# HGRN2 layer on one core: near-token products done elementwise and summed by a matmul with ones behind the value projections, and the K and Q updates of both directions in one operation each

## The chip, the cores and the metric

The kernel runs on one core of a Trainium2 chip. The metric is the device time of one execution in microseconds; the time before is the median of three runs. A profile shows one execution, and its span (first to last instruction) is slightly shorter than the time of the same run.

The engines that matter here are TensorE (PE in the profile, with its weight loads as PEld), VectorE (DVE), ScalarE (ACT), GpSimd (POOL) and the DMA queue that SyncE issues (SP).

## The reference

Two layers over 1024 latent tokens and 256 context tokens of width 1024. Layer 0 is a neighbourhood attention beside a bidirectional mLSTM and is not touched. Layer 1, where the change lies, is a bidirectional gated linear recurrence (HGRN2) with 16 heads of key and value width 128:

```python
def _c_mixer(h_lat, h_ctx, w_in, lb, h_norm, w_out, need_ctx):
    ...
        q, f_fwd, f_bwd, i, z = _split_cols(h @ w_in, C_SIZES)
        f = lb + (1.0 - lb) * jax.nn.sigmoid(f_pre.astype(F32))    # k = 1 - f, decay = f
    ...
def _gla_chunkwise(q, k, v, lf, S):            # per direction, in chunks
        b = jnp.cumsum(lfc, axis=2)
        o = jnp.einsum('bhtk,bhkv->bhtv', qc * jnp.exp(b), S)
        pair = jnp.exp(jnp.where(tri, b[:, :, :, None, :] - b[:, :, None, :, :], -jnp.inf))
        a = jnp.einsum('bhtk,bhtsk->bhts', qc, pair * kc[:, :, None, :, :])
        o = o + jnp.einsum('bhts,bhsv->bhtv', a, vc)
        S = jnp.exp(bL[:, :, 0])[..., None] * S + jnp.einsum('bhsk,bhsv->bhkv', kc * jnp.exp(bL - b), vc)
```

For a query token t and a key token s of one chunk the weight is a sum over the 128 key channels of q, k and the product of the decays between s and t. The outputs of both directions are added, normalised per head, gated by SiLU(z) and projected.

## The kernel before

Everything is float32 in memory. Dense projections are exact to about float32 by splitting both operands into a high and a low float32r part and doing three float32r passes for each 128 rows of the contraction (lines 117, 118 and 119); `split` (lines 71 and 72) makes the parts: ScalarE copies the high part, VectorE subtracts. The small matmuls of the recurrence are done in float32, and each of these shows as two passes on PE.

Layer 1 runs over the 16 heads, with these steps for each:

- `hg_proj` (from L756) projects the forget gates of both directions and q, transposed (channels on partitions, tokens along the row). `F` holds the decays of one half of the tokens (512), for both directions; `q` the queries.
- `hg_intra` (from L834) does the two halves, half 1 first. It builds `K` (1 - F, both directions, L841) and `Q` (q times F, both directions, L844), and then calls `hg_level` for seven levels. On level `lev` the blocks have h = 2^lev tokens; the block pairs on either side of a boundary are joined. ScalarE gathers the keys that look across the boundary into `ksel` (L875), TensorE multiplies them with the queries for each of the four chunks of 128 tokens (L880), and VectorE writes the result into `A` under a mask: by multiplication on level 0 (L886), by a predicated copy on the others (L890). Then VectorE moves K and Q on by one block of decay, by four operations on 256 elements (L898), and multiplies the block decays (L900).
- After level 0, `hg_diag` sets the diagonal of `A`: L888 adds the two directions of K, L909 multiplies with q on TensorE, L910 copies under the identity mask.
- At the end of `hg_intra`, K is transposed by TensorE (L859) and copied into `kn` (L861).
- `hg_vz` (from L782) projects the values and z: a context tile first, then eight tiles of 128 tokens (24 passes each, `wz` weights). `v` is copied by ScalarE (L799), z gets a sigmoid (L800) and is multiplied on VectorE (L801). The PSUM tiles of all projections share two buffers (`mm`), and the tile of z has one buffer, which the normalisation of the head before still reads (`gyn`, L953).
- `hg_ctx` builds the state that the context leaves (L810 to L829), and `hg_scan` passes over the eight chunks: backward states (L920, L922), then per chunk the three products that make the output (L932, L933, L934) and the forward state (L937, L939). After every four chunks ScalarE squares (L948), GpSimd takes the root (L142, L144), VectorE scales and gates (L953), TensorE transposes (L956), and ScalarE stores to `gyt` (L958), from where a DMA writes it out.

The framework orders the instructions of each engine when the kernel is built, by its own estimate of the times, and each engine then runs its list strictly in that order, waiting on semaphores. So projections are laid between the small matmuls of the recurrence: the value projections of a head between its levels, the gate and query projections of the next head between the steps of the scan. `t(pool, ..., tag, bufs)` takes a buffer of a tag; an operation that writes a buffer waits until its last reader is done.

Of the kernel before, what the change touches and what calls it, by code (L numbers as in the profile page):

```python
# [9 lines left out]
F32 = mybir.dt.float32  # L10
F32R = mybir.dt.float32r
U8 = mybir.dt.uint8
# [31 lines left out]
class Prog:  # L44
# [789 lines left out]
    def hg_intra(self, st, pool):  # L834
        nc = self.nc
        n = 512
        hv = {}
        for hf in (1, 0):
            F, q = st["F"][hf], st["q"][hf]
            K = self.t(pool, [P, 2, n], F32, "gK", 2)  # L840
            nc.vector.tensor_scalar(out=K, in0=F, scalar1=-1.0, scalar2=1.0, op0=ALU.mult, op1=ALU.add)  # L841
            Q = self.t(pool, [P, 2, n], F32, "gQ", 2)
            for d in range(2):
                nc.vector.tensor_tensor(out=Q[:, 1 - d, :], in0=q, in1=F[:, d, :], op=ALU.mult)  # L844
            A = self.t(pool, [P, 4, P], F32, "gA", 2)
            hv[hf] = dict(Q=Q, A=A, T=F, K=K)
        for lev in range(7):
            for hf in (1, 0):
                self.hg_level(hv[hf], lev, pool)
            if lev == 0:  # L850
                for hf in (1, 0):
                    self.hg_diag(hv[hf], st["q"][hf], pool)
        for hf in (1, 0):
            H = hv[hf]
            H["kn"] = []
            for d in range(2):
                p = self.ps("tr", [P, 4, P])
                for c in range(4):
                    nc.tensor.transpose(p[:, c, :], H["K"][:, d, c * P : (c + 1) * P], self.ident)  # L859
                k_ = self.t(pool, [P, 4, P], F32, "gkn", 4)  # L860
                nc.scalar.copy(k_, p)  # L861
                H["kn"].append(k_)
        return hv


    def hg_level(self, H, lev, pool):
        nc = self.nc
        n, h = 512, 1 << lev
        nb = n // (2 * h)
        K, Q, A, Tt = H["K"], H["Q"], H["A"], H["T"]  # L870
        sel = lambda t: t.rearrange("p d (b s i) -> p d b s i", s=2, i=h)

        pick = lambda t: _skew(t[:, 0, :].rearrange("p (b s i) -> p b s i", s=2, i=h), 2, n)
        ksel = self.t(pool, [P, n], F32, "gksel", 3)
        nc.scalar.copy(ksel.rearrange("p (b s i) -> p b s i", s=2, i=h), pick(K))  # L875
        qp = pick(Q)
        pa = self.ps("s", [P, 4, P])
        nbc = P // (2 * h)
        for c in range(4):
            nc.tensor.matmul(  # L880
                pa[:, c, :].rearrange("p (b s i) -> p b s i", s=2, i=h),
                lhsT=ksel[:, c * P : (c + 1) * P], rhs=qp[:, c * nbc : (c + 1) * nbc], start=True, stop=True,
            )
        if lev == 0:

            nc.vector.tensor_tensor(out=A, in0=pa, in1=self.lmask0.unsqueeze(1).to_broadcast([P, 4, P]), op=ALU.mult)  # L886
            H["ks"] = self.t(pool, [P, n], F32, "gksel", 3)
            nc.vector.tensor_tensor(out=H["ks"], in0=K[:, 0, :], in1=K[:, 1, :], op=ALU.add)  # L888
        else:
            nc.vector.copy_predicated(A, self.lmask[:, lev - 1, :].unsqueeze(1).to_broadcast([P, 4, P]), pa)  # L890
        Tv = Tt.rearrange("p d (b s) -> p d b s", s=2)
        bc = lambda t: t.unsqueeze(2).to_broadcast([P, nb, h])
        Kv, Qv = sel(K), sel(Q)
        for t, i, s, tot in (
            (Kv, 0, 0, Tv[:, 0, :, 1]), (Kv, 1, 1, Tv[:, 1, :, 0]),
            (Qv, 0, 0, Tv[:, 1, :, 1]), (Qv, 1, 1, Tv[:, 0, :, 0]),
        ):
            nc.vector.tensor_tensor(out=t[:, i, :, s, :], in0=t[:, i, :, s, :], in1=bc(tot), op=ALU.mult)  # L898
        Tn = self.t(pool, [P, 2, nb], F32, f"gT{lev}", 2)
        nc.vector.tensor_tensor(out=Tn, in0=Tv[:, :, :, 0], in1=Tv[:, :, :, 1], op=ALU.mult)  # L900
        H["T"] = Tn


    def hg_diag(self, H, q, pool):
        nc = self.nc
        pa = self.ps("s", [P, 4, P])
        for c in range(4):
            s = slice(c * P, (c + 1) * P)
            nc.tensor.matmul(pa[:, c, :], lhsT=H["ks"][:, s], rhs=q[:, s], start=True, stop=True)  # L909
        nc.vector.copy_predicated(H["A"], self.ident8.unsqueeze(1).to_broadcast([P, 4, P]), pa)  # L910

    def hg_scan(self, h, st, halves, S, pool, y):
        nc = self.nc
# [48 lines left out]
    def build(self):  # L962
        tc, nc, a = self.tc, self.nc, self.a
        dma = nc.sync.dma_start
        with ExitStack() as es:
# [130 lines left out]
            with tc.tile_pool(name="op0", bufs=2) as op, ExitStack() as wl:  # L1096
                self.gate_bc(0, op, 2, 1)
                later = []
                w1 = self.wo_half(wl, a["woab"], 0, "left", yp, later)
                for tt in [8, 9, 3, 4, 2, 5, 1, 6, 0, 7]:  # L1100
                    xt = self.t(op, [P, D], F32, "ox", 2)[:, 512:D]
                    self.out_tile(w2, 1, tt, self.yd, self.xin(tt), xt, yp, op, 2, part=acc[:, tt, :])
                    nc.gpsimd.dma_start(out=self.x1[tt * P : (tt + 1) * P, 512:D], in_=xt)
                    for ld in later[:2]:
                        ld()
                    later = later[2:]
                self.zero = self.t(lk, [P, CTX], F32, "gzero", 1)
                nc.vector.memset(self.zero, 0.0)
                self.lmask = self.t(lk, [P, 6, P], U8, "glm8", 1)
                self.lmask0 = self.t(lk, [P, P], F32, "glm0", 1)  # L1110
                self.ident8 = self.t(lk, [P, P], U8, "ident8", 1)
                nc.vector.tensor_copy(self.ident8, self.ident)
                lm = self.t(op, [P, D], F32, "nx", 1)[:, 0 : 7 * P].rearrange("p (l f) -> p l f", f=P)
                dma(out=lm, in_=a["glm"])
                nc.vector.tensor_copy(self.lmask, lm[:, 1:7, :])
                nc.vector.tensor_copy(self.lmask0, lm[:, 0, :])
                self.gate_bc(0, op, 2, 0)
                wr.close()
                right = es.enter_context(ExitStack())
                self.open_h(right)  # L1120
                self.wp = right.enter_context(tc.tile_pool(name="w1", bufs=2, side="right"))
                self.rawp = op
                self.slabs = 4
                wf = self.wring([a["wc"][:, 2048 : 2048 + P]], P)
                for tt in [8, 9, 4, 5, 6, 7, 0, 1, 2, 3]:
                    xt = self.t(op, [P, D], F32, "ox", 2)
                    dma(out=xt[:, 512:D], in_=self.x1[tt * P : (tt + 1) * P, 512:D])
                    self.out_tile(w1, 0, tt, self.yd, self.xin(tt), xt[:, 0:512], op, op, 2)
                    if tt < 8:
                        nc.gpsimd.dma_start(out=self.x1[tt * P : (tt + 1) * P, 0:512], in_=xt[:, 0:512])  # L1130
                    xn = self.t(op, [P, D], F32, "nx", 1)
                    self.norm(xn, xt, op)
                    self.mod_tr(1, [xn], tt, op, self.h_sink(tt * P, P))

            with l1:
                pool = l1.enter_context(tc.tile_pool(name="hg", bufs=2))
                self.rawp = pool
# [172 lines left out]
```

## Time and profile before

| what | value |
|---|---|
| time, median of 3 runs | 3584.57 us (3582.02 to 3586.4) |
| time of the profiled run | 3583.22 us |
| its span | 3581.4 us |
| PE busy | 3516.8 us (98%) |
| DVE busy | 2216.1 us (62%) |
| ACT busy | 1418.4 us (40%) |
| POOL busy | 454.6 us (13%) |
| mean granted TensorE clock | 0.992 |

In the timeline a row gives the start, the duration, the engine, the line and the tiles. The end of a matmul is modelled, and the next one starts before it: what a matmul takes of TensorE is read from the start of one to the start of the next (called its slot here), not from its duration. Operations on VectorE that do not depend on each other overlap a little in the same way.

### The profile page before, as it was taken

Reading aid. Unit: us, or ns where it says so; the run is one execution under the profiler, and the core shown is the slowest. Engines: PE = TensorE matmul, PEld = TensorE weight load, DVE = VectorE, ACT = ScalarE, POOL = GpSimd, SP = SyncE. Lnnn points to the kernel's source line nnn. Section 1 sums busy time; section 2 is a strip of 40 time slices with the busy share of each in tenths; the row PEclk is TensorE's granted clock in tenths of the full one; section 3 lists DMA queues with packets and bytes.
Section 4 is the critical chain, followed back from the end, with each engine's and each line's share of the span. In section 5 each row is a group of like instructions: output and inputs, shape, how many; then the busy total and the mean of one; then the engine's idle time right before and its main releaser. Section 6 shows DMA issues by size and latency. Waiting matters only on the chain.

```text
span 3581.4 us, 65599 instructions
## 1 busy us (share of the span) xinstructions
PE 3516.8 (98%) x24954; PEld 3222.6 (90%) x24954; DVE 2216.1 (62%) x5976; ACT 1418.4 (40%) x3493; POOL 454.6 (13%) x752
## 2 busy tenths in 40 slices
PE   8999999999999999998999999999999999999998
PEld 5879999999999999997788999999999999999877
DVE  4646676666754765664666666666666666666653
ACT  5545555445533434433354333333333333333341
POOL 2222222122211212211010000000000000000000
PEclk9999999999999999999999999999999999999999
DMA  5532323232234434324752111111111111110263
GB/s 206 175 103 75 84 70 84 72 89 75 79 96 148 127 93 141 118 72 141 228 158 62 36 36 36 33 36 36 36 35 34 31 36 36 35 33 27 74 205 116
DMA packets 323051, 305.25 MB, mean 85 GB/s; under 512 B 29016, under 2 KB 280088, under 8 KB 322608
## 3 DMA queue, kind: packets, MB, share of 16 engines
q1 hardware_dynamic: 290704, 217.44, 20.9%
q0 software_dynamic: 32032, 83.61, 6.9%
q8 instruction: 197, 3.23, 0.4%
q14 instruction: 118, 0.97, 0.1%
HBM read 241.49 MB, written 59.30 MB: 84 GB/s over the span
## 4 chain that ended last, share of the span: by engine, by line
PE 88%; issue 5%; DMA 3%; DVE 1%; ACT 1%; POOL 1%; SPq 0%; POOLq 0%; DVEq 0%; ACTq 0%
PE mm L119 18%; PE mm L117 18%; PE mm L118 18%; PE s L880 6%; PE mm L729 2%; PE mm L731 2%; PE mm L730 2%; PE acc L674 2%; PE tr L654 2%; PE acc L458 2%; PE s L467 2%; DMA mld<-md 1%; PE acc L448 1%; PE acc L933 1%; PE s L909 1%
## 5 line engine op out<-in xcount | busy, mean ns | idle before, releaser
L119 PE MATMUL mm<-wh,hl 128*128 128x256 f32 x2560 | 748.9, 293 | 0.2 <-DVE hl L250 0.2
L117 PE MATMUL mm<-wh,hh 128*128 128x256 f32 x2560 | 746.5, 292 | 0.0
L118 PE MATMUL mm<-wl,hh 128*128 128x256 f32 x2560 | 745.4, 291 | 0.0
L119 PEld LDWEIGHTS mm<-wh,hl 128*128 128x128 f32 x2560 | 488.5, 191 | 11.1 <-issue 4.1
L117 PEld LDWEIGHTS mm<-wh,hh 128*128 128x128 f32 x2560 | 488.6, 191 | 7.7 <-issue 1.4
L118 PEld LDWEIGHTS mm<-wl,hh 128*128 128x128 f32 x2560 | 488.7, 191 | 7.1 <-issue 0.8
L117 PE MATMUL mm<-hh,wh 128*128 128x512 f32 (+1 forms) x1216 | 449.5, 370 | 5.9 <-ACT gFc L769 5.9
L118 PE MATMUL mm<-hl,wh 128*128 128x512 f32 (+1 forms) x1216 | 449.2, 369 | 0.0
L119 PE MATMUL mm<-hh,wl 128*128 128x512 f32 (+1 forms) x1216 | 448.7, 369 | 0.0
L119 PE MATMUL mm<-wzh,hl 128*128 128x256 f32 x1024 | 295.3, 288 | 0.0
L117 PE MATMUL mm<-wzh,hh 128*128 128x256 f32 x1024 | 294.2, 287 | 0.0
L118 PE MATMUL mm<-wzl,hh 128*128 128x256 f32 x1024 | 293.9, 287 | 0.0
L875 ACT COPY gksel<-gK 128x512 f32<-128x512 f32 x224 | 148.8, 664 | 317.0 <-PE s L880 159.9
L117 PEld LDWEIGHTS mm<-hh,wh 128*128 128x128 f32 x1216 | 230.3, 189 | 37.5 <-ACT gFc L769 6.2
L119 PEld LDWEIGHTS mm<-hh,wl 128*128 128x128 f32 x1216 | 230.3, 189 | 31.7
L118 PEld LDWEIGHTS mm<-hl,wh 128*128 128x128 f32 x1216 | 230.3, 189 | 30.8
L880 PE MATMUL s<-gQ,gksel 128*128 128x128 f32 x1792 | 254.9, 284 | 0.0
L729 PE MATMUL mm<-woh,yh 128*128 128x512 f32 x576 | 229.8, 400 | 5.6 <-DVE oacc L743 3.5
L880 PEld LDWEIGHTS s<-gQ,gksel 128*128 128x128 f32 x1792 | 231.4, 191 | 1.3
L731 PE MATMUL mm<-woh,yl 128*128 128x512 f32 x576 | 229.6, 399 | 0.8 <-DVE yl L72 0.8
L730 PE MATMUL mm<-wol,yh 128*128 128x512 f32 x576 | 229.3, 398 | 0.4 <-DVE wol L72 0.2
L71 ACT CAST wh<-wraw 128x512 fp32r<-128x512 f32 x240 | 147.2, 619 | 202.8 <-PE mm L118 126.2
(307 smaller groups left out, 7349.6 us busy)
## 6 DMA issues: line engine op xcount, KB each, us to landing
wraw<-yd SPq DMA_DIRECT2D x144, 256.0 KB
wraw<-in_wab_dram SPq DMA_DIRECT2D x112, 256.0 KB
md<-ev POOLq DMA_DIRECT2D x100, 256.0 KB, 2.7
wraw<-in_wc_dram SPq DMA_DIRECT2D x96, 256.0 KB
adar<-in_wada_dram POOLq DMA_DIRECT2D x32, 512.0 KB, 4.8
wraw<-in_wc_dram SPq DMA_DIRECT2D x128, 128.0 KB
adar<-in_wada_dram SPq DMA_DIRECT2D x16, 512.0 KB
wraw<-in_wab_dram SPq DMA_DIRECT2D x64, 128.0 KB
```

The costliest lines, as they stand in the source:

```text
L71: nc.scalar.copy(hi, x)
L117: mm(ps, lhsT=lh(k), rhs=rh(k), start=(k == 0), stop=False)
L118: mm(ps, lhsT=lh(k), rhs=rl(k), start=False, stop=False)
L119: mm(ps, lhsT=ll(k), rhs=rh(k), start=False, stop=(k == nk - 1))
L458: nc.tensor.matmul(num, lhsT=qc[:, j, :], rhs=C[d][:, j, :], start=False, stop=(j == 1))
L467: nc.tensor.matmul(u, lhsT=st["k"][c][:, j * P : (j + 1) * P], rhs=vw, start=True, stop=True)
L654: nc.tensor.transpose(pt[:nk, i, :], pr[:, o : o + nk], self.ident)
L729: mm(ps, lhsT=yh[:, k, :], rhs=w.h(kk), start=(kk == 0), stop=False)
L730: mm(ps, lhsT=yh[:, k, :], rhs=w.l(kk), start=False, stop=False)
L731: mm(ps, lhsT=yl[:, k, :], rhs=w.h(kk), start=False, stop=(kk == 8 * len(qs) - 1))
L875: nc.scalar.copy(ksel.rearrange("p (b s i) -> p b s i", s=2, i=h), pick(K))
L880: nc.tensor.matmul(pa[:, c, :].rearrange("p (b s i) -> p b s i", s=2, i=h), lhsT=ksel[:, c * P : (c + 1) * P], rhs=qp[:, c * nbc : (c + 1) ...
```

## The change

The two nearest kinds of pairs, a token with its neighbour in a block of two (level 0) and a token with itself (the diagonal), no longer go through a float32 matmul.

- `hg_near`, called in `hg_intra` for each half, makes two tiles of 512 products: K of one direction times Q of the other for neighbours (L926 of the changed kernel; the operands alternate between the two directions from token to token), and (K0 + K1) times q for the token itself (L927 and L928). They take buffers of the tag `gkn`, which the transposed K used alone before.
- `hg_close`, called after `hg_vz`, splits each of the four tiles into float32r parts, multiplies both parts with a matrix of ones (two passes on 512 columns each, L864 and L865), which puts the sum over the 128 channels into every row, and copies them into `A` under the mask of level 0 or the identity (L867). The split uses the buffers `gsg` and `gyt`. The transposes of K move to its end (L874, L876).
- `hg_level` on level 0 only updates K, Q and the block decays; the first write of `A` is that of level 1, by multiplication (L901).
- K is updated in both directions by one operation on 512 elements, and so is Q (L911), where there were four on 256.
- The mask of level 0 becomes an 8-bit tile, and a tile of ones is made once.

```diff
@@ hg_intra @@
             hv[hf] = dict(Q=Q, A=A, T=F, K=K)
+            self.hg_near(hv[hf], q, pool)
         for lev in range(7):
             for hf in (1, 0):
                 self.hg_level(hv[hf], lev, pool)
-            if lev == 0:
-                for hf in (1, 0):
-                    self.hg_diag(hv[hf], st["q"][hf], pool)
+        return hv
+
+    def hg_close(self, hv, pool):
+        nc = self.nc
+        for i in range(2):
+            for hf in (1, 0):
+                H = hv[hf]
+                hi = self.t(pool, [P, 512], F32R, "gsg", 1)
+                lo = self.t(pool, [P, 512], F32R, "gyt", 1)
+                self.split(hi, lo, H["near"][i])
+                pa = self.ps("s", [P, 4, P])
+                p2 = pa.rearrange("p a b -> p (a b)")
+                nc.tensor.matmul(p2, lhsT=self.ones, rhs=hi, start=True, stop=False)
+                nc.tensor.matmul(p2, lhsT=self.ones, rhs=lo, start=False, stop=True)
+                mask = self.ident8 if i else self.lmask0
+                nc.vector.copy_predicated(H["A"], mask.unsqueeze(1).to_broadcast([P, 4, P]), pa)
...
@@ hg_level @@
-        if lev == 0:
-            nc.vector.tensor_tensor(out=A, in0=pa, in1=self.lmask0.unsqueeze(1).to_broadcast([P, 4, P]), op=ALU.mult)
-            H["ks"] = self.t(pool, [P, n], F32, "gksel", 3)
-            nc.vector.tensor_tensor(out=H["ks"], in0=K[:, 0, :], in1=K[:, 1, :], op=ALU.add)
-        else:
-            nc.vector.copy_predicated(A, self.lmask[:, lev - 1, :].unsqueeze(1).to_broadcast([P, 4, P]), pa)
+        if lev > 0:
...
+            mask = self.lmask[:, lev - 1, :].unsqueeze(1).to_broadcast([P, 4, P])
+            if lev == 1:
+                nc.vector.tensor_tensor(out=A, in0=pa, in1=mask, op=ALU.mult)
+            else:
+                nc.vector.copy_predicated(A, mask, pa)
         Tv = Tt.rearrange("p d (b s) -> p d b s", s=2)
-        bc = lambda t: t.unsqueeze(2).to_broadcast([P, nb, h])
-        Kv, Qv = sel(K), sel(Q)
-        for t, i, s, tot in (
-            (Kv, 0, 0, Tv[:, 0, :, 1]), (Kv, 1, 1, Tv[:, 1, :, 0]),
-            (Qv, 0, 0, Tv[:, 1, :, 1]), (Qv, 1, 1, Tv[:, 0, :, 0]),
-        ):
-            nc.vector.tensor_tensor(out=t[:, i, :, s, :], in0=t[:, i, :, s, :], in1=bc(tot), op=ALU.mult)
+        m = 2 * nb
+        for t, o, step in ((K, 1, m - 1), (Q, m + 1, -m - 1)):
+            v = bass.AP(t.tensor, t.offset, [list(t.ap[0]), [n + h, 2], [2 * h, nb], [1, h]])
+            tot = bass.AP(Tt.tensor, Tt.offset + o, [list(Tt.ap[0]), [step, 2], [2, nb], [0, h]])
+            nc.vector.tensor_tensor(out=v, in0=v, in1=tot, op=ALU.mult)
...
-    def hg_diag(self, H, q, pool):
-        nc = self.nc
-        pa = self.ps("s", [P, 4, P])
-        for c in range(4):
-            s = slice(c * P, (c + 1) * P)
-            nc.tensor.matmul(pa[:, c, :], lhsT=H["ks"][:, s], rhs=q[:, s], start=True, stop=True)
-        nc.vector.copy_predicated(H["A"], self.ident8.unsqueeze(1).to_broadcast([P, 4, P]), pa)
+    def hg_near(self, H, q, pool):
+        nc = self.nc
+        n = 512
+        K, Q = H["K"], H["Q"]
+        kx = bass.AP(K.tensor, K[:, 1, 1:n].offset, [list(K.ap[0]), [2, n // 2], [-(n + 1), 2]])
+        qx = bass.AP(Q.tensor, Q.offset, [list(Q.ap[0]), [2, n // 2], [n + 1, 2]])
+        pr = [self.t(pool, [P, n], F32, "gkn", 4) for _ in range(2)]
+        nc.vector.tensor_tensor(out=pr[0].rearrange("p (b s) -> p b s", s=2), in0=kx, in1=qx, op=ALU.mult)
+        nc.vector.tensor_tensor(out=pr[1], in0=K[:, 0, :], in1=K[:, 1, :], op=ALU.add)
+        nc.vector.tensor_tensor(out=pr[1], in0=pr[1], in1=q, op=ALU.mult)
+        H["near"] = pr
...
@@ build @@
-                self.lmask0 = self.t(lk, [P, P], F32, "glm0", 1)
+                self.lmask0 = self.t(lk, [P, P], U8, "glm0", 1)
+                self.ones = self.t(lk, [P, P], F32R, "ones", 1)
+                nc.vector.tensor_scalar(
+                    out=self.ones, in0=self.ident, scalar1=0.0, scalar2=1.0, op0=ALU.mult, op1=ALU.add
+                )
...
                     hv = self.hg_intra(st, pool)
                     self.hg_vz(h, st, pool)
+                    self.hg_close(hv, pool)
                     S = self.hg_ctx(st, pool)
```

More of the change, by code (lines that the diff above doesn't have):

```diff
@@ L859, in hg_intra @@
                     nc.tensor.transpose(p[:, c, :], H["K"][:, d, c * P : (c + 1) * P], self.ident)
-                k_ = self.t(pool, [P, 4, P], F32, "gkn", 4)
+                k_ = self.t(pool, [P, 512], F32, "gkn", 4).rearrange("p (a b) -> p a b", a=4)
                 nc.scalar.copy(k_, p)
                 H["kn"].append(k_)
-        return hv
     def hg_level(self, H, lev, pool):
@@ L870, in hg_level @@
         K, Q, A, Tt = H["K"], H["Q"], H["A"], H["T"]
-        sel = lambda t: t.rearrange("p d (b s i) -> p d b s i", s=2, i=h)
         pick = lambda t: _skew(t[:, 0, :].rearrange("p (b s i) -> p b s i", s=2, i=h), 2, n)
-        ksel = self.t(pool, [P, n], F32, "gksel", 3)
-        nc.scalar.copy(ksel.rearrange("p (b s i) -> p b s i", s=2, i=h), pick(K))
-        qp = pick(Q)
-        pa = self.ps("s", [P, 4, P])
-        nbc = P // (2 * h)
-        for c in range(4):
[L880 to L883, printed above, removed]
@@ L893, in hg_level @@
-        Kv, Qv = sel(K), sel(Q)
-        for t, i, s, tot in (
-            (Kv, 0, 0, Tv[:, 0, :, 1]), (Kv, 1, 1, Tv[:, 1, :, 0]),
-            (Qv, 0, 0, Tv[:, 1, :, 1]), (Qv, 1, 1, Tv[:, 0, :, 0]),
-        ):
-            nc.vector.tensor_tensor(out=t[:, i, :, s, :], in0=t[:, i, :, s, :], in1=bc(tot), op=ALU.mult)
+        if lev > 0:
+            ksel = self.t(pool, [P, n], F32, "gksel", 3)
+            nc.scalar.copy(ksel.rearrange("p (b s i) -> p b s i", s=2, i=h), pick(K))
+            qp = pick(Q)
+            pa = self.ps("s", [P, 4, P])
+            nbc = P // (2 * h)
+            for c in range(4):
+                nc.tensor.matmul(
+                    pa[:, c, :].rearrange("p (b s i) -> p b s i", s=2, i=h),
+                    lhsT=ksel[:, c * P : (c + 1) * P], rhs=qp[:, c * nbc : (c + 1) * nbc], start=True, stop=True,
+                )
[4 more added lines that the diff above has]
+                nc.vector.copy_predicated(A, mask, pa)
@@ L901, in hg_level @@
         H["T"] = Tn
-    def hg_diag(self, H, q, pool):
+    def hg_near(self, H, q, pool):
         nc = self.nc
-        pa = self.ps("s", [P, 4, P])
-        for c in range(4):
-            s = slice(c * P, (c + 1) * P)
-            nc.tensor.matmul(pa[:, c, :], lhsT=H["ks"][:, s], rhs=q[:, s], start=True, stop=True)
-        nc.vector.copy_predicated(H["A"], self.ident8.unsqueeze(1).to_broadcast([P, 4, P]), pa)
+        n = 512
[7 more added lines that the diff above has]
+        H["near"] = pr
     def hg_scan(self, h, st, halves, S, pool, y):
@@ L1109, in build @@
                 self.lmask = self.t(lk, [P, 6, P], U8, "glm8", 1)
-                self.lmask0 = self.t(lk, [P, P], F32, "glm0", 1)
+                self.lmask0 = self.t(lk, [P, P], U8, "glm0", 1)
                 self.ident8 = self.t(lk, [P, P], U8, "ident8", 1)
                 nc.vector.tensor_copy(self.ident8, self.ident)
+                self.ones = self.t(lk, [P, P], F32R, "ones", 1)
+                nc.vector.tensor_scalar(
+                    out=self.ones, in0=self.ident, scalar1=0.0, scalar2=1.0, op0=ALU.mult, op1=ALU.add
+                )
                 lm = self.t(op, [P, D], F32, "nx", 1)[:, 0 : 7 * P].rearrange("p (l f) -> p l f", f=P)
```

## The prediction

> **What bounds the kernel now.** I read the profile page first, then a window over the recurrent stage, then the timeline of one head.
>
> ```profile
> span 3581.4 us, 65599 instructions
> PE 3516.8 (98%) x24954; PEld 3222.6 (90%) x24954; DVE 2216.1 (62%) x5976; ACT 1418.4 (40%) x3493; POOL 454.6 (13%) x752
> PE   8999999999999999998999999999999999999998
> PEclk9999999999999999999999999999999999999999
> 1932.00:3372.50 1440.50, 1440.50 (x10178) 1345.94 (x10176) 948.48 (x2360) 466.34 (x1132) 64.07 (x90) 1.00 0.11 33
> ```
>
> The last line is the stage that the change touches, in the view of windows (busy time of PE, PEld, DVE, ACT, POOL, then the clock): TensorE is busy in all 1440.5 us, VectorE in 948. Busy is not proof, since a matmul's end is modelled, so I take starts. Two rows of the chain that ended last show the same step (level 0, half 1) in two heads that follow each other:
>
> ```profile
> 2406.40 1.00 PE s L880 x6
> 2498.60 1.00 PE s L880 x6
> ```
>
> One head takes 92.20 us. Between these marks I find no gap in PE's starts: every head is the sum of its matmul slots, and what leaves TensorE leaves the time, as long as its order finds each operand ready.
>
> **The change, part by part: TensorE.** These rows give the slots.
>
> ```profile
> 2405.09 0.40 PE L118 MATMUL mm<-hl,wh 128*128 128x512 f32 x1
> 2405.32 0.39 PE L119 MATMUL mm<-hh,wl 128*128 128x512 f32 x1
> ...
> 2411.14 0.28 PE L119 MATMUL mm<-hh,wzl 128*128 128x256 f32 x1
> ...
> 2413.15 0.28 PE L118 MATMUL mm<-wzl,hh 128*128 128x256 f32 x1
> 2413.26 1.49 PE L880 MATMUL s<-gQ,gksel 128*128 128x128 f32 x8
> 2414.58 0.61 PE L909 MATMUL s<-gq,gksel 128*128 128x128 f32 x4
> 2415.03 0.38 PE L956 MATMUL tr<-ident,gyn 128*128 128x128 f32 x2
> ```
>
> Eight passes of level 0 take 2414.58 - 2413.26 = 1.32 us, 0.165 each; four of the diagonal 0.45, 0.112 each, which I also use for all other float32 passes and transposes. A float32r pass takes 0.23 us on 512 columns and 0.118 on 256 (17 of them from 2411.14 to 2413.15). Removed for each head: 16 passes of level 0 (2.64) and 16 of the diagonal (1.79), 4.43 us. Added: eight passes on 512 columns with the ones, 1.84 us. Net 2.59 us, over 16 heads 41.4 us. This would be the gain if TensorE stayed full.
>
> **VectorE and ScalarE.** Per half and level, two pairs of 256 become two operations of 512.
>
> ```profile
> 2414.79 0.69 DVE L886 TENSOR_TENSOR gA<-s,glm 128x512 f32<-128x512 f32 x1 [1.70 <-PE s L880]
> 2415.40 0.75 DVE L898 TENSOR_TENSOR gQ<-gQ,gF 128x256 f32<-128x256 f32 x2
> 2416.06 0.60 DVE L953 SCALAR_TENSOR_TENSOR gyn<-acc,gss,gz 128x128 f32<-128x128 f32 x2
> 2416.58 0.75 DVE L898 TENSOR_TENSOR gK<-gK,gT 128x256 f32<-128x256 f32 x2
> 2417.25 0.73 DVE L910 COPY_PREDICATED gA<-ident,s 128x512 f32<-128x512 uint8 x1
> 2417.88 0.41 DVE L815 TENSOR_SCALAR gq<-gFc 128x512 f32<-128x512 f32 x1
> ```
>
> Starts again: an operation on 512 elements takes a slot of 0.61, a pair on 256 takes 0.66, a predicated copy 0.63, two `gyn` 0.52. So a merge saves 0.05, over 28 merges a head 1.4 us. The near products and the splits add ten operations of 0.61 and four predicated copies (L867), 8.6 us; L886, L888 and L910 of both halves go, 3.7. VectorE goes from 60.7 us a head (948.48 of 1440.5 us, times 92.2) to about 64, and ScalarE gains two copies net. Neither becomes the bound by its sum. These costs lie beside TensorE, except where TensorE waits for one; that place is the border between two heads.
>
> **The border.** The order of the changed program, as built, has in every steady head after the last output product (L953 of chunk 7, in place of L934):
>
> ```
> PE:  39 passes of 256 (rest of value tile 0, all of tile 1); transpose yn0; L794 twice;
>      transposes yn1, yn2, yn3; level 1 of half 0; level 2 of half 1; value tile 2
> DVE: L844 twice (half 0); L926; L927; L911 Q; gyn0, gyn1; L928; L911 K; gyn2, gyn3;
>      L813; L814; L911 K; L911 K; L816; L801 (tile 0)
> ```
>
> Value tile 2 needs the PSUM buffer of tile 0, which L801 frees; L801 and the sigmoid before it write the one z tile, so they stand behind the last `gyn` of the head before. In the old order level 0 and the diagonal lay in this stretch and filled it. Now I put numbers on it, from the end of that last product (2408.13 in the trace, where the next row starts):
>
> ```profile
> 2407.91 0.39 PE L934 MATMUL acc<-gS,gQ 128*128 128x128 f32 x2
> 2408.13 0.49 PE L880 MATMUL s<-gQ,gksel 128*128 128x128 f32 x2
> 2410.06 0.28 POOL L142 TENSOR_SCALAR gss<-gss 128x4 f32<-128x4 f32 x1 [5.90 <-ACT gjk L948]
> 2410.42 1.36 POOL L144 TENSOR_TENSOR gss<-gss,mhalf 128x4 f32<-128x4 f32 x1
> 2411.81 0.61 DVE L953 SCALAR_TENSOR_TENSOR gyn<-acc,gss,gz 128x128 f32<-128x128 f32 x2
> 2450.06 0.68 DVE L813 TENSOR_TENSOR_SCAN gEc<-gFc,gzero 128x255 f32<-128x255 f32 x1 [1.54 <-issue]
> 2450.66 0.66 DVE L814 TENSOR_TENSOR_SCAN gEc<-gFc,gzero 128x255 f32<-128x255 f32 x1
> 2451.24 0.26 DVE L801 TENSOR_TENSOR gz<-gz,mm 128x128 f32<-128x128 f32 x1
> 2414.79 0.67 ACT L875 COPY gksel<-gK 128x512 f32<-128x512 f32 x1 [2.96 <-PE s L880]
> ```
>
> - VectorE: the squares and the root allow `gyn0` at 2411.81 - 2408.13 = 3.68. Before it come L844 twice, L926, L927 and L911: 0.2 (the hop that the L886 row shows after PE) + 5 x 0.61 + 0.1 = 3.35, covered. Then two `gyn` to 4.20, L928 to 4.81, K to 5.42, two `gyn` to 6.02, the scans (0.60 and 0.58) to 7.20, two K updates to 8.42, L816 to 9.02, L801 done at 9.30.
> - TensorE: 39 x 0.118 = 4.60, four small passes to 5.05. yn3 is ready at 6.1, and the selected keys of half 0 (K done at 5.5, ScalarE copy 0.67) at 6.15. The level groups, due at 5.27 if nothing waited, start at 6.27: a wait of 1.0. They take 16 x 0.112 = 1.79, to 8.06. Value tile 2 starts at 9.36: a wait of 1.3.
>
> So the border gives back 2.3 of the 2.59 us. The rest of the head I followed in the same way: the first `gyn` group is ready some 0.3 us before its transposes, the levels have 0.7 us or more to spare after the wait, the last float32r sums 4 us. Queued behind L801 on VectorE are only level updates with that spare time; ScalarE's copies of the split stand between weight casts and delay no projection in this count. The lower split of the first near sum also waits on VectorE for the store of `gyt`; it is reached after that has landed.
>
> For L926 the trace has no VectorE operand that jumps between two rows from element to element. ScalarE has one, the gathering copy of level 0:
>
> ```profile
> L875 ACT COPY gksel<-gK x224: 607/621/878, 1932.1 to 3360.0; 128x512 f32<-128x512 f32 x112
> ```
>
> Its longest, 878 ns, are those; the median is 621. So L926 costs 0.61 at least and 0.61 x 1.41 = 0.86 at most; I take 0.86, and the border does not feel it: 3.35 + 0.25 is under 3.68. The Trainium skill, page "SBUF — State Buffer", section "Door 1: The DMA port swizzle", says that consecutive accesses within one 16-byte line run at full rate and each access to a new line pays; that speaks against this operand and agrees with the 878 ns. By it the sum would be the same as long as the payment stays below 0.33 us.
>
> **First and last head.** Head 0 has no border ahead and keeps its 2.59. For the last one, everything of `hg_close` follows the last value tile:
>
> ```profile
> 3372.56 0.63 PE L820 MATMUL tr<-ident,gq 128*128 128x128 f32 x4
> 3380.30 0.80 PE L729 MATMUL mm<-woh,yh 128*128 128x512 f32 x1
> ```
>
> The 7.7 us up to the first output pass hold little work of TensorE, so its new 3.6 us fit. VectorE's four predicated copies and three subtractions (4.4 us) stand among the casts of the output weights: 0 to 4.4 us, I take 1.5, nearer to hidden, as that stretch waits for weights from memory too.
>
> **Sum.** 16 x 2.59 - 15 x 2.3 - 1.5 = 5.4 us less. The profiled run took 3583.2 us (1.4 below the median of 3584.57): 3578.
>
> **Rivals.**
>
> *A: the border does not wait.* TensorE stays full: 3583.2 - 41.4 + 1.5 = 3543. For it: today not one gap in the stage, and the framework lays the order so that by its own estimate operands are there. Against it: the 39 passes are all that its two PSUM buffers allow, whatever the estimate.
>
> *B: the wait for value tile 2 is longer, and the result slower.* The place is VectorE's list from `gyn0` to L801. No operation with the pattern of L911 (two directions, blocks, broadcast decay) is in the trace. Nearest are the slots 0.61 and 0.66 above; the far bound is again x 1.41, 0.86. Three of them are in the list: +0.75 us a head. If seven operations there also wait for each other's end (0.69 instead of 0.61), +0.56. Slower by over 0.2% begins at +0.8 a head; both together give 3578 + 15 x 1.31 = 3598. A longer wait then reaches the clock:
>
> ```profile
> 1273.45:1276.86 3.41, 1.79 (x15) 1.53 (x15) 1.82 (x6) 2.01 (x7) 0.00 (x0) 1.00 0.63 203
> 1276.86:1280.27 3.41, 3.41 (x31) 3.41 (x31) 0.19 (x1) 1.35 (x4) 0.73 (x1) 1.00 0.66 192
> 1734.30:1737.70 3.40, 1.68 (x6) 1.14 (x7) 3.40 (x6) 3.40 (x7) 0.00 (x0) 1.00 0.82 234
> 1737.70:1741.10 3.40, 3.40 (x9) 2.67 (x9) 3.40 (x7) 1.85 (x4) 0.19 (x1) 0.50 0.86 251
> ```
>
> After a window of 3.4 us with 1.68 us busy the next ran at half clock, after one with 1.79 it did not. At the border I count about 1.9 to 2.2 busy, since the level groups lie between the two waits; a wait of about 2 us at tile 2 passes the mark and costs 1.7 us more, at most 3598 + 25 = 3623. The Trainium skill, page "TensorE: Matmul & The Clock Gate", section "Why this matters for your kernels", sets the mark at idle gaps of about 3 us; by it no wait here would touch the clock and B would end at 3598. The rows decide for the lower mark.
>
> **How the numbers follow.** Forecast 0.58, A 0.15, B 0.27. The forecast's own range: each hop is known to some 0.3 us a head, 5 us, with the tail 3571 to 3590. The range 3568 to 3608 leaves out A and the halved clock of B (about 0.05). Under 0.2% (7 us, about what a measurement of this kernel can tell from none) lies most of the forecast: same 0.42; faster 0.15 + 0.10; slower 0.27 + 0.06.
>
> **What would show it.** One head at 91.9 us; TensorE idle about 1.0 us before level 1 of half 0 and 1.3 before the third value tile, released by VectorE (L801); eight ones passes at 0.23 starts; L911 at 0.61. Wrong, if a head takes 89.6 (A) or over 92.8 (B), or if TensorE waits in `hg_close`.

## The result, and the profile after

The changed kernel takes 3589.07 us (median of 18 runs, 3585.07 to 3593.62), and the kernel before 3582.94 us on the same chips: 1.0017 times as long, 95% interval 1.0010 to 1.0024. The forecast was 5.4 us less; measured are 6.1 us more. The page of the changed kernel: span, engines with busy time, then PE and its clock in 40 slices.

```profile
span 3585.9 us, 64319 instructions
PE 3494.6 (97%) x24570; PEld 3183.6 (89%) x24570; DVE 2265.7 (63%) x5657; ACT 1422.3 (40%) x3525; POOL 455.5 (13%) x752
PE   8999999999999999998999999999999999999998
PEclk9999999999999999999999999999999999999999
```

The view of windows over its recurrent stage (length, busy PE, PEld, DVE, ACT, POOL, clock, DMA share, GB/s):

```profile
1925.00:3367.70 1442.70, 1415.38 (x9779) 1304.73 (x9778) 994.56 (x2034) 468.82 (x1158) 64.13 (x90) 1.00 0.11 33
```

TensorE does less and is no longer busy all the time: 27.3 us of the stage are idle, where there were none. In the chain that ended last the same step (the root of one group) returns after 92.50 us; before it was 92.20.

```profile
2408.16 0.51 POOL gss L142
...
2500.66 0.51 POOL gss L142
```

The border between two heads, first VectorE and then TensorE, in the timeline (start, duration, engine, line, tiles; in brackets the idle time and what ended it):

```profile
2406.44 1.29 DVE L844 TENSOR_TENSOR gQ<-gq,gF 128x512 f32<-128x512 f32 x2 [0.67 <-PE acc L953]
2407.76 0.84 DVE L926 TENSOR_TENSOR gkn<-gK,gQ 128x512 f32<-128x512 f32 x1
...
2410.14 0.61 DVE L972 SCALAR_TENSOR_TENSOR gyn<-acc,gss,gz 128x128 f32<-128x128 f32 x2 [0.32 <-POOL gss L144]
2410.66 0.68 DVE L928 TENSOR_TENSOR gkn<-gkn,gq 128x512 f32<-128x512 f32 x1
2411.26 0.69 DVE L911 TENSOR_TENSOR gK<-gK,gF 128x512 f32<-128x512 f32 x1
2411.87 0.62 DVE L972 SCALAR_TENSOR_TENSOR gyn<-acc,gss,gz 128x128 f32<-128x128 f32 x2
...
2413.58 1.27 DVE L911 TENSOR_TENSOR gK<-gK,gT 128x512 f32<-128x512 f32 x2
2414.76 0.69 DVE L816 TENSOR_TENSOR gq<-gq,gEc 128x512 f32<-128x512 f32 x1
2415.37 0.48 DVE L801 TENSOR_TENSOR gz<-gz,mm 128x128 f32<-128x128 f32 x2
```

```profile
2406.01 0.39 PE L953 MATMUL acc<-gS,gQ 128*128 128x128 f32 x2
...
2411.24 0.27 PE L975 MATMUL tr<-ident,gyn 128*128 128x128 f32 x1
2412.27 0.33 PE L975 MATMUL tr<-ident,gyn 128*128 128x128 f32 x1 [0.76 <-DVE gEc L811]
...
2412.71 2.12 PE L894 MATMUL s<-gQ,gksel 128*128 128x128 f32 x16
2415.80 0.36 PE L117 MATMUL mm<-wzh,hh 128*128 128x256 f32 x1 [0.97 <-DVE gz L801]
```

Two gaps, as drawn in the forecast. From the second transpose of `gyn` to the third there are 1.03 us from start to start instead of 0.11. The releaser is named as the memset L811, whose tile this transpose does not read: it needs the third `gyn`, which started at 2411.87. The third value tile starts 1.24 us after the last L894 product did, and is released by L801. Counted as what exceeds a usual slot of 0.11, these are 0.92 and 1.13 us; three passes behind the first gap have slots that are too long by 0.33 us together, so the border loses 2.4 us a head. L801 starts 2415.37 - 2406.01 = 9.36 us after the last output product.

Three groups of instructions of the changed kernel from 1970 to 3365 us (line, shape, count, busy time, mean ns of one), and where TensorE waited at the end of the stage, after and, second, before:

```profile
L926 DVE TENSOR_TENSOR gkn<-gK,gQ 128x512 f32<-128x512 f32 x30 | 25.3, 842 | 0.5
L864 PE MATMUL s<-gsg,ones 128*128 128x512 f32 x60 | 24.2, 403 | 0.0
L865 PE MATMUL s<-gyt,ones 128*128 128x512 f32 x60 | 23.6, 393 | 0.0
```

```profile
PE s L864 <- ACT gsg L71: 3.8, 2, 2.3
PE mm L729 <- ACT yh L71: 2.8, 1, 2.8
PE mm L731 <- DVE yl L72: 1.5, 1, 1.5
```

```profile
PE s L920 <- DVE gS L922: 2.8, 3, 1.5
PE mm L729 <- DVE oacc L743: 1.9, 1, 1.9
PE s L827 <- ACT gknc L822: 0.7, 1, 0.7
PE mm L731 <- DVE yl L72: 0.4, 1, 0.4
```

In the steady heads no ones pass waits (0.0 idle before L864 and L865). In the last head they do, for the split on ScalarE, 3.8 us; and the output projection then waits longer for the last `y`. The granted clock falls there too. Two stretches at half clock in the view of windows (the clock is third from the end), again after and, second, before:

```profile
3374.70:3381.50 6.80, 5.76 (x16) 4.61 (x17) 6.80 (x12) 6.75 (x13) 0.00 (x0) 0.50 1.01 313
3449.80:3456.60 6.80, 6.00 (x14) 4.75 (x15) 4.80 (x9) 2.04 (x4) 0.54 (x1) 0.50 1.00 301
```

```profile
3379.50:3382.90 3.40, 3.25 (x9) 2.71 (x10) 3.29 (x8) 2.65 (x5) 0.00 (x0) 0.50 1.05 352
3447.80:3451.20 3.40, 3.40 (x10) 2.63 (x9) 3.40 (x7) 2.48 (x5) 0.00 (x0) 0.50 0.84 235
```

These are 13.6 us at half clock in place of 6.8, in one profile each; in the profiles of the other kernels without the near sums it is 6.8 to 10.2.

### The profile page after: what moved, and what is told of

It reads as the page before. It is cut to its first block, busy times and chain, and to the rows that moved or that the text cites. A ratio compares the mean times of both kernels' runs of the same rounds, so it can differ in the third digit from the quotient of the medians.

```text
span 3585.9 us, 64319 instructions
## 1 busy us (share of the span) xinstructions
PE 3494.6 (97%) x24570; PEld 3183.6 (89%) x24570; DVE 2265.7 (63%) x5657; ACT 1422.3 (40%) x3525; POOL 455.5 (13%) x752
## 4 chain that ended last, share of the span: by engine, by line
PE 83%; issue 6%; DVE 3%; DMA 3%; POOL 1%; ACT 1%; SPq 0%; POOLq 0%; ACTq 0%; DVEq 0%
PE mm L117 17%; PE mm L119 17%; PE mm L118 17%; PE s L894 4%; PE mm L731 2%; PE mm L729 2%; PE mm L730 2%; PE acc L674 2%; PE tr L654 2%; PE s L467 2%; PE acc L458 2%; PE acc L448 1%; DMA mld<-md 1%; PE acc L953 1%; PE acc L951 1%
## 5 line engine op out<-in xcount | busy, mean ns | idle before, releaser
L117 PE MATMUL mm<-wzh,hh 128*128 128x256 f32 x1024 | 302.2, 295 | 14.5 <-DVE gz L801 14.5
L72 DVE TENSOR_TENSOR wl<-wraw,wh 128x512 fp32r<-128x512 f32 x240 | 164.0, 689 | 96.0 <-ACT wh L71 94.5
L117 PEld LDWEIGHTS mm<-wzh,hh 128*128 128x128 f32 x1024 | 194.4, 190 | 16.9 <-PE s L894 16.9
L894 PE MATMUL s<-gQ,gksel 128*128 128x128 f32 x1536 | 204.0, 277 | 0.0
```

The lines of the kernel that those rows point to most:

```text
L72: nc.vector.tensor_tensor(out=lo, in0=x, in1=hi.bitcast(F32), op=ALU.subtract)
L117: mm(ps, lhsT=lh(k), rhs=rh(k), start=(k == 0), stop=False)
L894: nc.tensor.matmul(pa[:, c, :].rearrange("p (b s i) -> p b s i", s=2, i=h), lhsT=ksel[:, c * P : (c + 1) * P], rhs=qp[:, c * nbc : (c + 1) ...
```

## The experiments

Each time is a median, each ratio is to the kernel before on the same chip, with its 95% interval. "Head" is the period of a steady head in the trace.

| kernel | us | ratio | head, us |
|---|---|---|---|
| changed kernel | 3589.07 | 1.0017 (1.0010 to 1.0024) | 92.50 |
| z_halves | 3571.92 | 0.9959 (0.9947 to 0.9972) | 91.24 |
| z_halves_old | 3586.59 | 0.9999 (0.9991 to 1.0008) | 92.27 |
| updates_only | 3588.20 | 1.0003 (0.9995 to 1.0012) | 92.31 |
| near_only | 3602.99 | 1.0047 (1.0034 to 1.0061) | 92.99 |
| pad_before | 3591.20 | 1.0016 (1.0007 to 1.0025) | 92.55 |
| after_even | 3584.56 | 0.9995 (0.9986 to 1.0004) | 92.19 |
| z_halves_gyn4 | 3552.43 | 0.9905 (0.9891 to 0.9918) | 90.15 |
| last_early | 3589.13 | 1.0004 (0.9995 to 1.0012) | 92.50 |
| pad_wz_only, pad_64, pad_192 | 3589.01, 3582.76, 3588.37 (one run each) | | 92.50, 92.11, 92.44 |
| old_z_gyn4 | 3590.70 | 1.0013 (1.0004 to 1.0023) | 92.27 and 92.72 in turn |
| gyn4_one_gate | 3551.20 | 0.9909 (0.9893 to 0.9926) | 90.15 |
| best_even | 3549.29 | 0.9904 (0.9889 to 0.9919) | 90.02 |

### The wait behind L801: two gate tiles

```
-        z = self.t(pool, [P, NT - 2, P], F32, "gz", 1)
+        z = [self.t(pool, [P, 4, P], F32, f"gz{i}", 1) for i in range(2)]
```

> The changed kernel with the gate z in two tiles (value tiles 0 to 3, and 4 to 7) in place of one, so that the gates of the first four value tiles no longer stand behind the last gyn of the head before; nothing else. Theory (the border between heads holds the loss: 1.03 us behind the last gyn and 1.24 us behind L801, 2.4 with the small ones, in each of 15 heads): the order can now put value tiles 2 to 4 into the border, a head goes from 92.5 to about 90.1 us, and the time to 3589 - 36 = 3553 us (ratio to the kernel before 0.990 to 0.993). Rival 1 (the wait for gyn stays and only the one behind L801 goes): a head of 91.2, 3570 us. Rival 2 (the loss is in slower passes, not in waits): 92.3 or more a head, 3586 to 3589 us.

> Control: the kernel before with the same two gate tiles. It has no gap at the border, so all theories of the border expect the time of the kernel before, 3583 us within 4, and 92.2 us a head. If it gains 10 us or more, the gain of the split gate is not the border's wait of the changed kernel.

The first rival came out: 91.24 us a head (91.2 expected) and 3572 us (3570). L801 of the next head no longer stands behind the last `gyn`, its wait is gone, and one slot of 1.28 us before a transpose of `gyn` stays:

```profile
2408.70 0.33 PE L976 MATMUL tr<-ident,gyn 128*128 128x128 f32 x1 [1.01 <-DVE gyn L973]
```

The period of 91.24 us holds from the fourth border on; the first three show no such wait. The control without the near change gains nothing.

### The two halves of the change

`updates_only` puts the second line into the kernel before; `near_only` puts the first back into the changed kernel.

```
-for t, i, s, tot in (...):                 # four operations of 256 columns
+for t, o, step in ((K, 1, m - 1), (Q, m + 1, -m - 1)):   # two of 512
```

> The kernel before with only the second part of the change: K and Q updates of both directions in one operation each of 512 columns; level 0 and the diagonal stay matmuls. Theory (VectorE is off the path there, and an update of 512 columns takes a slot of about 0.61 us): same as before, 3583 us within 4, a head 92.2. Rival B of the prediction (the operand over two directions, blocks and a broadcast decay costs 0.86): VectorE grows by 28 x 0.2 = 5.6 us a head, still below TensorE, the level groups wait, 3590 us or more. If the float32r passes slow down here from 0.229 to 0.2297 us (0.4 us a head, 3589 us), the merged operands are what slows them.

> The changed kernel with the four old updates of 256 columns: only the near products and their sums by ones are new. Theory: the whole of the change's effect on TensorE is here; the border's VectorE list has three updates that take 0.66 in place of 0.61, so its wait is 0.15 us longer, a head 92.6 to 92.7 us and 3589 + 2 = 3591 us within 4. If the merged updates had cost time in the changed kernel (rival B), this would be faster than 3585 us.

Alone, the merged updates change nothing that can be told (1.0003). The second expectation missed: 3603 us, where 3591 was expected. The merges that are worth nothing alone are worth some 11 us beside the near sums, because VectorE's list at the border decides there. In the traces 15 heads take 11.4 us more than in the changed kernel (1401.5 against 1390.1, from the end of one head's value projections to that of the next). A steady head is 0.49 us longer. L801 starts 9.56 us after the last product in place of 9.36, and TensorE, whose order also shifted, comes to the first `gyn` transpose earlier, 4.66 us after the product in place of 4.90. The first border in `near_only` cost more: that head takes 98.17 us, where the changed kernel takes 93.42. View of windows of `near_only` (busy PE first, the clock third from the end):

```profile
2044.86:2048.27 3.41, 0.94 (x7) 0.49 (x5) 3.15 (x9) 0.64 (x2) 1.75 (x2) 1.00 0.00 0
2048.27:2051.69 3.42, 2.77 (x13) 2.68 (x14) 3.42 (x12) 2.73 (x6) 0.60 (x1) 0.50 0.00 0
2051.69:2055.10 3.41, 3.41 (x18) 3.41 (x18) 3.41 (x10) 1.24 (x2) 0.00 (x0) 0.50 0.20 77
```

and its waits of TensorE in this stretch:

```profile
PE tr L978 <- DVE gyn L975: 2.0, 1, 2.0
PE tr L978 <- DVE gEc L811: 1.1, 1, 1.1
```

A window with 0.94 us busy is followed by two at half clock, each of which can do some 1.7 us less (an estimate: half of 3.4). The longest single wait there is 2.0 us. The Trainium skill, page "TensorE: Matmul & The Clock Gate", section "Why this matters for your kernels", warns of idle gaps over about 3 us. Here a shorter one and part of a second in one window were enough. Page and measurement differ, so the windows decide, as rival B of the forecast had it.

### The place of the value weights

The value tiles' passes on 256 columns, 118.2 ns each in the kernel before, took 119.6 in the changed one. The built programs show what else had moved: the ones add 512 bytes to each partition and the near mask shrinks by 384, so all tiles of the stage lie 128 bytes further, the value weights (`wzh`, which is streamed) at byte 94,528 and no longer at 94,400.

```
 self.zero = self.t(lk, [P, CTX], F32, "gzero", 1)
+gap = self.t(lk, [P, 32], F32, "gap", 1)        # pad_before; then memset once
```

```
-self.zero = self.t(lk, [P, CTX], F32, "gzero", 1)
+self.zero = self.t(lk, [P, 1], F32, "gzero", 1)  # after_even; read as a broadcast
+gap = self.t(lk, [P, 216], F32, "gap", 1)
```

> The kernel before with one unused tile of 128 bytes a partition (32 float32, set to 0 once) ahead of the recurrent stage's tiles; no other edit. The changed kernel moves all these tiles by the same 128 bytes (the ones add 512, the near mask shrinks by 384), so the value weights start at byte 94,528 of a partition, not 94,400. Theory of placement: the value projection's passes of 256 columns go from 118.0 to 120.0 ns as in the changed kernel, 192 of them a head, so a head takes 92.2 + 0.4 = 92.6 us and the time is 3583 + 6 = 3589 us (ratio 1.0012 to 1.0025). Rival (the passes are slowed by what VectorE and ScalarE do beside them in the changed kernel): a head of 92.2 and the time of the kernel before within 3 us.

> The changed kernel with the zeros of the context scan read from one column (a broadcast) and the freed space refilled so that the stage's tiles lie where they lay before the change (value weights at byte 94,400). Theory of placement: passes of 256 columns at 118.0 ns again, a head 92.5 - 0.4 = 92.1 us, 3589 - 6 = 3583 us. Rival (slowed by VectorE and ScalarE): a head of 92.5, 3589 us.

Placement is confirmed both ways: 128 unused bytes make the kernel before slower by as much as the whole change did (1.0016), and the changed kernel with its tiles in the old place is level with the kernel before (0.9995). Then other places, one run each, by `gap` tiles of 16 and 48 float32 in the kernel before, and by one of 32 that is allocated just ahead of `wz`:

```
+if h == 0:
+    gap = self.t(pool, [P, 32], F32, "gap", 1)          # pad_wz_only
 w = self.wblock(pool, "wz", [col(3), col(4)], KD, 256)
```

> The kernel before with the 128 unused bytes placed behind the keys, queries and gates of the stage, so that only the value weights and what follows them (values, gate) lie 128 bytes further. Theory (it is the address of the streamed value weights that counts): passes of 256 columns in the value tiles take 120.0 ns and a head 92.5 to 92.6 us, as with all tiles moved. Rival (it is the keys, queries or the selected keys whose place counts): 118.0 ns and 92.2 us.

> The kernel before with 64 unused bytes ahead of the stage: value weights at byte 94,464, that is 0 above a multiple of 256 (before: 192; changed kernel: 64). If a start on a line of 256 bytes is best, 118.0 ns or less and a head of 92.2 us or less; if any other start than that of the kernel before is bad, 120.0 ns and 92.55 us.

> The same with 192 bytes: value weights at byte 94,592, 128 above a multiple of 256. If what counts is the place within 256 bytes in steps of 128, this lies like pad_64 (0 and 128 alike); if it changes from place to place without that, the passes tell by how much: 118.0 ns is 92.2 us a head, 120.0 ns is 92.55 us.

Ten passes of a value tile, first and eleventh start in the timeline, of the kernel before, of `pad_64` and of `pad_wz_only`:

```profile
2432.59 0.28 PE L119 MATMUL mm<-wzh,hl 128*128 128x256 f32 x1
...
2433.77 0.28 PE L117 MATMUL mm<-wzh,hh 128*128 128x256 f32 x1
```

```profile
2433.39 0.28 PE L117 MATMUL mm<-wzh,hh 128*128 128x256 f32 x1
...
2434.55 0.28 PE L118 MATMUL mm<-wzl,hh 128*128 128x256 f32 x1
```

```profile
2432.47 0.28 PE L119 MATMUL mm<-wzh,hl 128*128 128x256 f32 x1
...
2433.67 0.28 PE L117 MATMUL mm<-wzh,hh 128*128 128x256 f32 x1
```

1.18, 1.16 and 1.20 us. Moving the value weights and what follows them is enough. The mean over the 161 to 172 undisturbed passes of a head in which `wz` streams, by the start of `wzh` above a multiple of 256 bytes:

| start | kernels | ns a pass |
|---|---|---|
| 0 | pad_64, best_even | 117.0, 117.1 |
| 192 | before, updates_only, z_halves_old, after_even | 118.2 each |
| 96 | z_halves_gyn4, gyn4_one_gate | 118.5 |
| 128 | pad_192 | 118.7 |
| 224 | old_z_gyn4 | 119.5 |
| 64 | changed, z_halves, pad_before, pad_wz_only, near_only | 119.6 to 119.9 |

Kernels as different as `near_only` and `pad_before` agree where the place agrees, so it is not what VectorE and ScalarE do beside. Of the expectations, the first branch for `pad_64` came out (a start on a multiple of 256 is best, 92.11 us a head); the thought that steps of 128 decide was wrong, 0 and 128 differ by 1.7 ns. That the pattern repeats every 256 bytes is not shown: only the first row holds two different addresses (94,464 and 93,696). Why a place is slow was not found.

### The wait before the third gyn: four buffers

With two `gyn` buffers the order puts L928 and L911 between the second and the third `gyn`, whose buffer a transpose has yet to free. The scan's zeros are read from one column, to make the space.

```
-yn = self.t(pool, [P, P], F32, "gyn", 2)
+yn = self.t(pool, [P, P], F32, "gyn", 4)
```

> The changed kernel with the gate in two tiles and four buffers for gyn in place of two (the zeros of the scan from one column, for the space). In the kernel with two gate tiles one wait is left in the border, 1.28 us before a transpose of gyn, a head 91.23. Theory (the four gyn of a group stand apart on VectorE because the third needs the buffer that a transpose has yet to free; with four buffers they stand together): the wait falls to 0.3 or less, a head 90.0 to 90.3 us, 3572 - 15 = 3557 us (ratio to the kernel before 0.990 to 0.993). Rival (the wait is the root and the squares ahead of gyn, not its buffers): a head of 91.2, 3572 us.

> The changed kernel with four gyn buffers and the single gate tile (the scan's zeros from one column, for the space; value weights 96 above a multiple of 256). If the waits are independent, the 1.03 us before the gyn transposes go and the 1.24 us behind L801 stay: a head 92.5 - 1.0 - 0.3 (place) = 91.2 us and 3571 us. If the time saved is waited for again behind L801, which then stands no earlier on VectorE, a head of 92.0 us or more and 3582 us or more.

> Control to z_halves_gyn4: the kernel before with the same two gate tiles, four gyn buffers and the scan's zeros from one column. It has no wait in the border to lose, so 92.2 to 92.6 us a head (its value weights start 224 above a multiple of 256, a place not yet seen) and 3583 to 3590 us. If it falls to 3565 us or less, the edit pays without the near sums, and the gain of 34 us of z_halves_gyn4 is not that of the passes the change removes.

The theory held in the first (3552 us, a head of 90.15), and the second overthrew my picture of two independent waits: four buffers give the same 90.15 us with the gate in one tile. Of the 2.35 us that a head gains, some 0.2 us are the place of the value weights, which moved along (118.5 in place of 119.6 ns a pass). VectorE in `gyn4_one_gate`, and then TensorE:

```profile
2400.00 1.29 DVE L844 TENSOR_TENSOR gQ<-gq,gF 128x512 f32<-128x512 f32 x2 [0.55 <-PE acc L953]
...
2403.70 1.13 DVE L972 SCALAR_TENSOR_TENSOR gyn<-acc,gss,gz 128x128 f32<-128x128 f32 x4 [0.32 <-POOL gss L144]
2404.74 0.68 DVE L928 TENSOR_TENSOR gkn<-gkn,gq 128x512 f32<-128x512 f32 x1
2405.34 0.68 DVE L911 TENSOR_TENSOR gK<-gK,gF 128x512 f32<-128x512 f32 x1
2405.94 0.28 DVE L801 TENSOR_TENSOR gz<-gz,mm 128x128 f32<-128x128 f32 x1
```

```profile
2405.60 0.49 PE L975 MATMUL tr<-ident,gyn 128*128 128x128 f32 x3
2406.28 0.39 PE L117 MATMUL mm<-wzh,hh 128*128 128x256 f32 x1 [0.19 <-DVE gz L801]
```

The four `gyn` stand together, and L801 comes 5.94 us after L844 began, in place of 8.93: the order lets scans and K updates stand behind it. TensorE's order moved as well: 46 passes on 256 columns, in place of 39, stand between the last product and the first of these transposes. A slot of 0.46 us instead of 0.11, 0.35 us too long, is the one gap that is left in the border. The control, with both edits on the old matmuls, is slower than the kernel before, not faster, and with 3590.70 us just above its expected range; its value weights lie in a slow place (119.5 ns). So the edits pay nothing by themselves: the gain needs the passes that the change removes.

### The last head, and the sum of the two causes

```
+if h == 15:
+    self.hg_close(hv, pool)                # last_early
 self.hg_vz(h, st, pool)
-self.hg_close(hv, pool)
+if h < 15:
+    self.hg_close(hv, pool)
```

```
+gap = self.t(lk, [P, 40], F32, "gap", 1)   # best_even: z_halves_gyn4 with this
-s = self.t(pool, [P, P], F32, "gS1", 10)
+s = self.t(pool, [P, P], F32, "gS1", 9)
```

> The changed kernel, where the last head alone makes its near sums ahead of its value projection (hg_close before hg_vz); the other heads are as they were. Theory (the near sums of the last head have nothing beside them and TensorE waits 2.08 and 2.74 us between the ones passes, and half the clock follows): those 4.8 us go, 3589 - 5 = 3584 us, up to 3 us less if the halved clock goes too. Rival (the waits at the end are those of the output weights and only change their place): 3589 us.

> The kernel z_halves_gyn4 with its tiles moved 160 bytes, so that the value weights start on a multiple of 256 (the place that gave 117.0 ns in pad_64); the space comes from nine in place of ten buffers of backward states. Theory of placement, additive to the border: 192 passes a head fall from 118.5 to 117.0 ns, a head 90.15 - 0.29 = 89.9 us, 3552 - 4.5 = 3548 us. If a wait of the border takes it back, 90.15 us and 3552 us.

`last_early` is at 1.0004, some 4.7 us better than the changed kernel's 1.0017, with intervals that overlap. Its time fits, its mechanism only in part: TensorE still waits at the end of the stage, though less and elsewhere. Its two longest waits:

```profile
PE acc L951 <- DVE gA L867: 2.5, 1, 2.5
PE mm L729 <- ACT yh L71: 1.2, 1, 1.2
```

The later wait of the output projection for the last `y` shrank from 2.8 to 1.2 us. With three small ones (1.9 us) the waits add up to 5.6 us, where the changed kernel has 8.1, and one of its two stretches of 6.8 us at half clock is gone. From the first gate projection to the end the profile takes 1690.9 us, in the changed kernel 1697.5. What the tail's order would be worth at best stays open. In `best_even` passes fell to 117.1 ns as expected; the head gained 0.13 us of the expected 0.29, and a gap longer by 0.05 us and some 120 passes on 512 columns, each about half a nanosecond slower, took back the larger part of the rest. Its time is not to be told from that of the other two kernels with four buffers and the near sums. All three beat the kernel before, by 0.9 to 1.0%.

## Why the prediction was wrong

**Right: what is removed and added.** In `gyn4_one_gate` a head without its 0.35 us of waits is 89.80 us; less 0.1 for the place of its weights (192 passes, 118.5 against 118.2 ns, and some at the edges) 89.7. The net is 2.5 us a head, forecast 2.59. The ones passes take slots of 0.23 to 0.24 us.

**Right in place and size, the cause only in part: the border.** Forecast were waits of 1.0 us behind `gyn` and 1.3 behind L801, and measured are 0.92 and 1.13, with 0.33 in the passes behind the first. In VectorE's list the second pair of `gyn` was counted as 0.60 where the rows give 0.52; this changes nothing. Counted from the end of the last product, where the next pass starts (2406.16), L801 starts at 9.21 us and with its 0.26 us ends at 9.47; forecast was 9.30. With the tiles in the old place a head is 92.19 us, so the border gives back 92.19 - 89.7 = 2.5, forecast 2.3. I had named the single gate tile as what holds L801 back. Splitting it removes that wait (`z_halves`), but is not needed: with four `gyn` buffers and one gate tile both waits go, so it was the two buffers, which the forecast does not mention, that put both there.

**Right: VectorE.** L926 takes 842 ns (taken 0.86 us at most); no wait comes from it. The merged updates stand 0.59 us apart (2413.58 to 2414.76 for two). The mechanism of rival B, a costly L911 and dependent operations, was not at work. The Trainium skill, page "SBUF — State Buffer", section "Door 1: The DMA port swizzle", says that each access that crosses to a new 16-byte line pays. The trace agrees in direction: L926 takes 842 ns, an operation of the same size on rows in order 690.

**Wrong, and the step that failed.** "A float32r pass takes 0.23 us on 512 columns and 0.118 on 256" was used as if the change could not touch the passes that it leaves alone. It moved their weights by 128 bytes, and the passes on 256 columns took 119.6 ns in place of 118.2: 92.50 - 92.19 = 0.31 us a head (192 passes make 0.27 of it), some 5 us in all. No rival held this. It is the largest term of the 11.5 us by which the forecast missed, and without it, in `after_even`, the change is level with the kernel before (0.9995, 0.9986 to 1.0004).

**Mis-sized.** Net and border together were each a little worse than forecast, 0.28 us a head (92.19 against 91.91), 4 us in all. First and last head were taken as a gain of 2.59 - 1.5 = 1.1 us. In the profiles the time from the first gate projection to the end grew by 8.6 us (1688.9 to 1697.5), and 15 heads, from the end of one head's value projections to that of the next, by 6.55 (1383.54 to 1390.09): the rest grew by 2.0, so the tail's term is about 3 us larger than 1.5. The forecast took it from VectorE's copies alone and had no term for the clock: 6.8 us more at half clock cost up to 3.4 us (an estimate from the windows above). That these two are the same 3 us is not shown. `hg_close` of the last head does wait, 3.8 us, which the forecast had listed as a sign of an error. Another 2 us lie in the first and the last border, which cost more than a steady one (6.55 against 15 x 0.30 = 4.5). Together 5 + 4 + 3 + 2 = 14 us, which is what these two profiles miss the forecast by (8.6 + 5.4); by the medians it is 11.5. The last two terms come from one profile each.

**Luck.** That 3589 lies within 3571 to 3590, the forecast's own range, is luck: its width stood for hops known to 0.3 us a head, and not for slower passes.

**Rival A** (3543 us, no wait) is what four buffers nearly reach, 3551 us: the order was as given, and the number of `gyn` buffers was part of what had made it so.

## What to carry to other kernels

Work taken off the bounding engine paid here only once the stretch that it had filled had something else to run. When a new wait appears, look at how many buffers the waiting chain has before splitting tiles, as more buffers can change the whole order (here two more, 1 KB a partition, took the ratio from 1.0017 to 0.9909, some 0.1% of it by the place of the weights). A new constant moves everything allocated behind it: compare the slots of untouched instructions before and after, and pad to the old place before blaming the new code. Two edits that are neutral or bad alone (1.0003 and 1.0047) need not add: measure them together and apart.

## What was not expected of the hardware

A float32r pass that streams 256 columns took between 117.0 and 119.9 ns by the place of the streamed tile (0 and 64 bytes above a multiple of 256; the values and gates, which lie behind it, moved along), while those that stream 512 columns of the unmoved `hh` stayed between 228.6 and 229.7. For 192 such passes a head this makes half a microsecond between the best and the worst place; measured are 92.11 us a head in `pad_64` and 92.55 in `pad_before`.
